# A small extra store of the first K block into the output, early in a linear attention kernel

## The chip, the cores and the metric

The kernel runs on one core of a Trainium2 chip. The metric is the device time of one execution in microseconds (us). A core has five engines with instruction queues of their own: TensorE (PE in the profile, with its weight loads as PEld), VectorE (DVE), ScalarE (ACT), GpSimd (POOL) and SyncE (SP). Data moves between the device memory (HBM) and the on-chip memory (SBUF) by 16 DMA engines. In this kernel SyncE and GpSimd issue the transfers; the profile lists those of SyncE under the queue q1 (hardware_dynamic) and those of GpSimd under q0 (software_dynamic).

## The reference

Linear attention without a mask, for 8 x 12 = 96 heads of 512 positions with 64 values each, all in float32:

```python
Q_feat = np.maximum(0, Q) + 1
K_feat = np.maximum(0, K) + 1
KV = np.einsum('bhkd,bhkv->bhdv', K_feat, V)
K_sum = np.sum(K_feat, axis=2)
numerator = np.einsum('bhqd,bhdv->bhqv', Q_feat, KV)
denominator = np.einsum('bhqd,bhd->bhq', Q_feat, K_sum)
return numerator / (denominator[:, :, :, None] + 1e-10)
```

Q, K, V and the output have 12.58 MB each, so 37.75 MB are read and 12.58 MB written.

## The kernel before

The 49,152 rows of 64 values are cut into blocks. A block of K or V has 128 partitions of 32 rows (8 heads). Two such blocks and the Q rows that belong to them make what the code calls a pair: 16 heads, and there are six of them, numbered s = 0 to 5. For each pair and each of its blocks n = 0, 1 the work is:

- `load` (line 135): GpSimd issues a DMA that reads K or V as float32 and writes bf16 tiles; `load_q` (line 131) does the same for Q. One exception is the first K block: `load_first_k` (line 125) lets SyncE load it in float32, as it is, into a buffer of the output pool `out_pool`, which nothing else uses yet.
- `k_features` (line 156): VectorE makes the K features, and `v_block` (line 169) on VectorE or ScalarE puts the V rows into a block layout with a column of ones, so that sums and products come out of one matmul.
- `keys_values` (line 181): 32 matmuls sum up KV and K_sum in PSUM; `weights` (line 194) brings them to SBUF as bf16.
- `q_features` (line 173), `transposes` (line 203) and `transposed` (line 210): Q features, transposed on TensorE and copied out.
- `out_matmuls` (line 215) and `norms` (line 229): the output matmuls, then a reciprocal (line 234) and a product (line 235) on VectorE into an output tile `o_sb`, in eight parts for each pair.
- `store` (line 148): the output tile goes to HBM. The stores of pairs 0 to 4 are issued by GpSimd, those of pair 5 by SyncE in three pieces.

The order on each engine is written out by hand in `ORDER` (line 23). A word there is a task: `lv2` is the load of V for pair 2, `s00` the first store of pair 0, `n31` part 1 of the norms of pair 3. GpSimd's list and SyncE's list are these:

```python
    POOL="""
        lv2 lk2 lq2 lv3 lq3 lk3 lq4 lv4 lk4 lv5 lq5 lk5 s00 s20 s10 s30 s40 s41
    """,
    SP="""
        s50 s51 s52
    """,
```

The loads of pairs 0 and 1 stand ahead of these lists, in the main part of the kernel (line 359 on). It begins with the first K block on SyncE, then V on GpSimd, then a few constants and the other loads. Semaphores are placed by the framework: an instruction waits for whatever last wrote what it reads, and for whoever last used the place that it writes. Output buffers rotate: `out_pool` has `OUT_BUFS` = 4, the first K block takes the first of them, pairs 0, 1 and 2 the next three, and pair 3 comes back to the first. `o_dram` (line 85) is the output seen as 128 partitions x 48 blocks x 8 rows x 64 values; eight of the 48 blocks belong to a pair.

Of the kernel before, what the change touches and what calls it, by code (L numbers as in the profile page):

```python
# [20 lines left out]
    k="kv", t="tr", m="om", f="kf", v="vb", q="qf", n="no", c="tc", e="ev", s="st"  # L21
# [32 lines left out]
def kernel(  # L54
# [12 lines left out]
    nc = tc.nc  # L67
# [11 lines left out]
    def view(t, c):  # L79
        return t.flatten_outer_dims().rearrange("(n p c) d -> p n c d", p=P, c=c)  # L80
# [4 lines left out]
    o_dram = view(out, C)  # L85
# [29 lines left out]
    raw = {}  # L115
# [9 lines left out]
    def load_first_k():  # L125
        t = out_pool.tile([P, 8, C, D], FP32, name="o_sb")
        t = t.rearrange("p a c d -> p (a c) d")[:, 0:ROWS]
        nc.sync.dma_start(out=t, in_=k_dram[:, 0])
        raw["k", 0, 0] = t

    def load_q(s):
        raw["q", s] = pools["q"].tile([P, QROWS, D], BF16, name="q_raw")
        nc.gpsimd.dma_start(out=raw["q", s], in_=q_dram[:, s])  # L133

    def load(x, s, ns=(0, 1)):
        if x == "q":
            load_q(s)
            return
        if (x, s) not in tiles:
            tiles[x, s] = pools[x].tile([P, 2, ROWS, D], BF16, name=f"{x}_raw")  # L140
        t = tiles[x, s]
        nc.gpsimd.dma_start(  # L142
            out=t[:, ns[0] : ns[-1] + 1], in_=drams[x][:, 2 * s + ns[0] : 2 * s + ns[-1] + 1]
        )
        for n in ns:
            raw[x, s, n] = t[:, n]
# [95 lines left out]
    def masks():  # L242
        nc.vector.tensor_scalar(out=odd, in0=lane, scalar1=16, scalar2=None, op0=ALU.bitwise_and)
        nc.vector.tensor_scalar(
            out=least[:, 0:1], in0=odd, scalar1=-1.0 / 16, scalar2=1.0, op0=ALU.mult, op1=ALU.add
        )
        nc.vector.tensor_scalar(
            out=least[:, 1:2], in0=odd, scalar1=1.0 / 16, scalar2=None, op0=ALU.mult
        )
        nc.vector.tensor_scalar(  # L250
            out=shift, in0=least, scalar1=-1.0, scalar2=-LOWEST, op0=ALU.add, op1=ALU.mult
        )
        nc.vector.tensor_tensor(out=shift, in0=shift, in1=least, op=ALU.add)

    def clear(i):
        t = v_alls[i].rearrange("p c x -> p (c x)").bitcast(FP32)
        w = t.shape[1] * 5 // 8
        nc.vector.memset(t[:, 0:w], 0.0)  # L258
        nc.scalar.copy(out=t[:, w:], in_=zero.to_broadcast([P, t.shape[1] - w]))  # L259
        nc.vector.tensor_copy(  # L260
            out=v_alls[i].rearrange("p c (b d) -> p c b d", b=4)[:, :, :, D],
            in_=ones[:, None, :].to_broadcast([P, ROWS, 4]),
        )
# [79 lines left out]
    def read(word):  # L343
        if word[0] == "l":
            return ("load", int(word[2]), word[1])
        return (TASKS[word[0]], *map(int, word[1:]))

    def trace_all(orders):

        left = {engine: list(tasks) for engine, tasks in orders.items()}  # L350
        while any(left.values()):
            before = len(done)
            for engine, tasks in left.items():
                while tasks and all(t in done or t[1] < 0 for t in needs(engine, tasks[0])):
                    trace(engine, tasks[0])
                    done.add(tasks.pop(0))
            assert len(done) > before, {e: t[:1] for e, t in left.items()}

    with tc.manual_schedule():
        nc.vector.memset(zero, 0.0)  # L360
        load_first_k()
        load("v", 0, (0,))
        nc.gpsimd.iota(lane, pattern=[[0, 1]], base=0, channel_multiplier=1)
        load("k", 0, (1,))
        load("v", 0, (1,))
        load("q", 0)
        nc.vector.memset(ones, 0.0)
        for b in range(4):
            nc.vector.memset(ones[32 * b : 32 * b + 32, b : b + 1], 1.0)
        clear(0)  # L370
        masks()
        make_identity(nc, identity)
        for t in kva_rows:
            nc.scalar.copy(out=t.bitcast(FP32), in_=zero.to_broadcast([P, 8 * W]))  # L374
        for x in "kvq":
            load(x, 1)
        clear(1)
        for s in range(2):
            done.update(("load", s, x) for x in "kvq")
        trace_all({engine: [read(x) for x in text.split()] for engine, text in ORDER.items()})  # L380
# [30 lines left out]
```

## Time and profile before

| what | value |
|---|---|
| time, median of 3 runs (lowest, highest) | 125.58 us (125.2, 126.08) |
| the profiled execution: time / span | 125.6 us / 123.8 us |
| mean granted TensorE clock | 0.901 |
| busy over the span | PE 83.0 us (67%), PEld 62.7 (51%), DVE 89.7 (72%), ACT 89.3 (72%), POOL 18.6 (15%) |
| HBM read and written | 37.75 MB and 12.58 MB |
| first load of K, issued by SyncE | at 0.74 us, lands after 4.8 us |
| loads issued by GpSimd | from 1.28 to 72.45 us |
| stores issued by GpSimd | from 73.47 to 108.73 us |
| stores issued by SyncE | from 112.10 to 115.46 us |

The profile shows one execution; its span runs from the first instruction to the last, and the rest of its time lies outside. A time in a slice row is given as a digit, the busy share in tenths, 40 slices over the span. The DMA row is the mean busy share of the 16 DMA engines, and the row GB/s what they moved, counted at the destination.

### The profile page before, as it was taken

The numbers are of one execution on the slowest core, as the hardware profiler recorded it, in microseconds if no ns is written. First come the engines' busy times: TensorE is split into PE (matmuls) and PEld (weight loads), VectorE is DVE, ScalarE is ACT, GpSimd is POOL, SyncE is SP. The second block draws the span as 40 slices with busy tenths as digits, with TensorE's granted clock in tenths as the row PEclk, the third lists the DMA queues.
The fourth block names the chain that finished last, engine by engine and source line by source line (L and its number), as shares of the span: only waits on it lengthen the run. The fifth ranks groups of instructions, "written<-read, shape, count | busy, mean of one in ns | idle before, by whom it ended". The sixth has DMA issues, their size and how long they took to land.

```text
span 123.8 us, 2306 instructions
## 1 busy us (share of the span) xinstructions
PE 83.0 (67%) x960; PEld 62.7 (51%) x960; DVE 89.7 (72%) x167; ACT 89.3 (72%) x99; POOL 18.6 (15%) x32
## 2 busy tenths in 40 slices
PE   0000396881998957999919998399984999976000
PEld 0000275851676835688716776277853677654000
DVE  4795429609699599969569992999959789789200
ACT  7959914939969999399999559999992996540000
POOL 6900000600003200140000090050000200220000
PEclk9999999999599997699995999999999599997555
DMA  3999999999999999999999999999999999999992
GB/s 85 339 212 212 217 214 217 213 232 220 192 212 217 229 209 209 214 220 210 220 226 198 213 217 216 213 226 202 214 327 417 419 413 418 417 413 417 409 407 100
DMA packets 7897, 32.11 MB, mean 259 GB/s; under 512 B 464, under 2 KB 464, under 8 KB 6992
## 3 DMA queue, kind: packets, MB, share of 16 engines
q0 software_dynamic: 6672, 28.84, 93.6%
q1 hardware_dynamic: 1216, 3.15, 6.8%
q8 instruction: 7, 0.11, 0.3%
q14 instruction: 2, 0.02, 0.0%
HBM read 37.75 MB, written 12.58 MB: 406 GB/s over the span
## 4 chain that ended last, share of the span: by engine, by line
DMA 44%; DVE 14%; PE 14%; ACT 13%; issue 4%; POOL 3%; POOLq 0%
DMA k_raw<-in_K_dram 32%; DMA q_raw<-in_Q_dram 12%; PE kva_ps L186 10%; DVE o_sb L235 7%; ACT v_all L171 6%; ACT qt L213 5%; DVE kf L159 4%; PE o_ps L221 3%; ACT kva L198 2%; POOL v_raw L142 2%; DVE v_all L171 2%; DVE recip L234 1%; PE qt_ps L206 1%; DVE qf L175 1%; POOL q_raw L133 0%
## 5 line engine op out<-in xcount | busy, mean ns | idle before, releaser
L186 PE MATMUL kva_ps<-v_all,kf 128*128 128x260 bf16 x384 | 55.2, 297 | 20.7 <-DVE v_all L171 17.7
L186 PEld LDWEIGHTS <-kf 128*128 128x128 bf16 x384 | 37.7, 105 | 31.1 <-DVE v_all L171 16.3
L171 ACT COPY v_all<-v_raw 32x2048 bf16<-32x2048 bf16 x22 | 42.3, 1929 | 6.9 <-DMA v_raw<-in_V_dram 5.1
L235 DVE TENSOR_TENSOR o_sb<-o_ps,recip 128x512 f32<-128x512 f32 x48 | 33.2, 692 | 1.7
L213 ACT COPY qt<-qt_ps 128x1024 bf16<-128x1024 bf16 x24 | 23.5, 1014 | 10.9 <-PE qt_ps L206 8.3
L221 PE MATMUL o_ps<-kva,qt 128*64 128x130 bf16 x384 | 20.6, 238 | 9.6 <-DVE o_sb L235 9.0
L159 DVE TENSOR_SCALAR kf<-k_raw,shift,least 128x2048 bf16<-128x2048 bf16 x22 | 16.9, 810 | 8.0 <-DMA k_raw<-in_K_dram 8.0
L221 PEld LDWEIGHTS <-qt 128*64 128x64 bf16 x384 | 13.3, 116 | 18.0 <-DVE o_sb L235 11.9
L171 DVE COPY v_all<-v_raw 32x2048 bf16<-32x2048 bf16 x26 | 18.0, 692 | 5.9 <-DMA v_raw<-in_V_dram 5.3
L198 ACT CAST kva<-kva_ps 64x260 bf16<-64x260 f32 x48 | 17.9, 374 | 3.7 <-PE kva_ps L186 2.9
L206 PE MATMUL qt_ps<-identity,qf 128*128 128x128 bf16 x192 | 14.0, 220 | 1.1 <-ACT qt L213 0.6
L206 PEld LDWEIGHTS <-qf 128*128 128x128 bf16 x192 | 12.0, 99 | 2.5 <-issue 0.8
L142 POOL DMA_DIRECT2D v_raw<-in_V_dram x7 | 4.9, 701 | 49.1 <-ACT qt L213 18.1
L234 DVE RECIPROCAL recip<-o_ps 128x8 f32<-128x8 f32 x48 | 9.6, 201 | 3.2 <-PE o_ps L221 3.0
L175 DVE TENSOR_SCALAR qf<-q_raw 128x4096 bf16<-128x4096 bf16 x6 | 7.3, 1223 | 4.7 <-DMA q_raw<-in_Q_dram 4.6
L150 POOL DMA_DIRECT2D out_dram<-o_sb x6 | 5.1, 853 | 30.9 <-DVE o_sb L235 23.6
L258 DVE MEMSET v_all<- 128x2600 f32 x2 | 4.5, 2225 | 1.1 <-issue 1.1
L133 POOL DMA_DIRECT2D q_raw<-in_Q_dram x6 | 3.5, 580 | 10.5 <-DVE recip L234 10.5
L142 POOL DMA_DIRECT2D k_raw<-in_K_dram x6 | 4.5, 746 | 0.0
L259 ACT COPY v_all<-zero 128x1560 f32<-128x1560 f32 x2 | 3.0, 1488 | 0.0
L159 DVE TENSOR_SCALAR kf<-o_sb,shift,least 128x2048 bf16<-128x2048 f32 x2 | 2.6, 1358 | 0.0
L374 ACT COPY kva<-zero 128x1040 f32<-128x1040 f32 x2 | 2.0, 1052 | 0.0
(17 smaller groups left out, 4.6 us busy)
## 6 DMA issues: line engine op xcount, KB each, us to landing
out_dram<-o_sb POOLq DMA_DIRECT2D x4, 2048.0 KB, 22.8
q_raw<-in_Q_dram POOLq DMA_DIRECT2D x6, 1024.0 KB, 17.4
k_raw<-in_K_dram POOLq DMA_DIRECT2D x5, 1024.0 KB, 19.9
v_raw<-in_V_dram POOLq DMA_DIRECT2D x5, 1024.0 KB, 15.7
out_dram<-o_sb POOLq DMA_DIRECT2D x2, 1024.0 KB, 10.0
o_sb<-in_K_dram SPq DMA_DIRECT2D x1, 1024.0 KB, 4.8
v_raw<-in_V_dram POOLq DMA_DIRECT2D x2, 512.0 KB, 8.5
out_dram<-o_sb SPq DMA_DIRECT2D x1, 1024.0 KB, 8.3
```

Of the source, the lines that this page charges most:

```text
L142: nc.gpsimd.dma_start(out=t[:, ns[0] : ns[-1] + 1], in_=drams[x][:, 2 * s + ns[0] : 2 * s + ns[-1] + 1])
L150: engine.dma_start(out=o_dram[:, 8 * s + lo : 8 * s + hi], in_=outs[s][:, lo:hi], single_packet=engine is nc.gpsimd,)
L159: nc.vector.tensor_scalar(out=kf[:, :, a], in0=raw["k", s, n], scalar1=shift[:, a : a + 1], scalar2=least[:, a : a + 1], op0=ALU.add, op1= ...
L171: copy(out=v_alls[n][ps, :, b * D1 : b * D1 + D], in_=raw["v", s, n][ps])
L175: nc.vector.tensor_scalar(out=qf.rearrange("p r c d -> p (r c) d"), in0=raw["q", s], scalar1=1.0, scalar2=1.0, op0=ALU.add, op1=ALU.max,)
L186: nc.tensor.matmul(kva_pss[s, n], lhsT=kfs[s, n][:, c].rearrange("p a d -> p (a d)"), rhs=v_alls[n][:, c], start=(c == 0), stop=(c == ROWS ...
L198: nc.scalar.copy(out=kvas[s % 2][64 * x : 64 * x + 64, 8 * n + a : 8 * n + 8 : 2, x], in_=kva_ps[64 * a : 64 * a + 64].rearrange("p (b d) ...
L206: nc.tensor.transpose(qt_ps[:, r], qfs[s][:, r, 2 * i : 2 * i + 2].rearrange("p x d -> p (x d)"), identity)
L213: copy(out=qts[s][:, i], in_=qt_pss.pop((s, i)).rearrange("p r q -> p q r"))
L221: nc.tensor.matmul(o_ps[64 * t : 64 * t + 64, c // 2, (c % 2) * W : (c % 2) * W + W], lhsT=qts[s][:, c, 8 * h : 8 * h + 8], rhs=kvas[s % 2 ...
L234: nc.vector.reciprocal(out=recip, in_=cells[:, :, :, D:D1])
L235: nc.vector.tensor_tensor(out=outs[s][:, part].rearrange("p (b r) d -> p b r d", b=2), in0=cells[:, :, :, 0:D], in1=recip.to_broadcast([P, ...
```

## The change

One line is added in the main part of the kernel, behind the first two loads. SyncE issues a DMA that copies from SBUF to the output: 16 partitions of the first K block, two rows of 64 float32 values from each, 512 B in one piece, 8 KB in all. The destination is partitions 0 to 15, block 0, rows 0 and 1 of the output, which belong to pair 0; what stands there is replaced when pair 0's own store writes the whole block.

```diff
         nc.vector.memset(zero, 0.0)
         load_first_k()
         load("v", 0, (0,))
+        nc.sync.dma_start(out=o_dram[0:16, 0, 0:2], in_=raw["k", 0, 0][0:16, 0:2])
         nc.gpsimd.iota(lane, pattern=[[0, 1]], base=0, channel_multiplier=1)
         load("k", 0, (1,))
         load("v", 0, (1,))
```

The instructions of the changed program differ from those before in these places alone: SyncE has the new DMA, which waits for the load of the first K block; GpSimd's store of pair 0 (line 150) waits for the new DMA; and one product on VectorE (line 235), the first into the output tile of pair 3, waits for it too. The order of all other instructions on each engine is as it was.

## The prediction

> **What bounds the kernel now.** I read first the 40 slices of the span, to see whether any engine or the transfers are full all the time; then the stretches, to see how full, and where that begins and ends; then the queues and the DMA issues, to price one packet and to find landing times. The slices:
>
> ```profile
> DVE  4795429609699599969569992999959789789200
> ACT  7959914939969999399999559999992996540000
> DMA  3999999999999999999999999999999999999992
> GB/s 85 339 212 212 217 214 217 213 232 220 192 212 217 229 209 209 214 220 210 220 226 198 213 217 216 213 226 202 214 327 417 419 413 418 417 413 417 409 407 100
> ```
>
> VectorE and ScalarE have holes in many slices; the DMA row is at 9 in all but the first and the last. The table by stage sharpens this (columns: the stretch in us, its length, busy us and instructions of PE, PE weight loads, DVE, ACT and POOL, the granted clock, the DMA share, GB/s):
>
> ```profile
> 0.00:3.00 3.00, 0.00 (x0) 0.00 (x0) 1.43 (x7) 2.25 (x2) 1.83 (x8) 1.00 0.35 74
> 3.00:20.00 17.00, 5.14 (x36) 3.79 (x37) 10.57 (x16) 11.76 (x9) 3.22 (x7) 1.00 1.05 238
> 60.00:80.00 20.00, 15.11 (x177) 11.30 (x175) 14.99 (x27) 16.78 (x19) 3.35 (x4) 0.91 1.05 214
> 95.00:115.00 20.00, 17.74 (x220) 12.53 (x216) 17.60 (x41) 12.13 (x18) 2.42 (x3) 0.87 1.02 415
> 115.00:121.00 6.00, 0.00 (x0) 0.00 (x0) 0.43 (x1) 0.00 (x0) 0.00 (x0) 0.50 1.03 406
> 121.00:122.00 1.00, 0.00 (x0) 0.00 (x0) 0.00 (x0) 0.00 (x0) 0.00 (x0) 0.50 0.52 201
> 122.00:123.80 1.80, 0.00 (x0) 0.00 (x0) 0.00 (x0) 0.00 (x0) 0.00 (x0) 0.50 0.02 9
> ```
>
> From 3 to 121 us the 16 DMA engines are full (a share of 1.02 to 1.05). The last compute instruction ends at 114.74 + 0.69 = 115.4 us, and 6 us of queued transfers still run behind it. The two rates are one limit seen twice: the loads are counted by the bf16 that they write, so 214 GB/s written is about 430 GB/s read, while a store counts the same on both sides and shows 415. A wait on a compute engine therefore costs nothing unless it leaves the DMA engines without work; what costs time is anything that occupies a DMA engine. The queue's own prices:
>
> ```profile
> DMA packets 7897, 32.11 MB, mean 259 GB/s; under 512 B 464, under 2 KB 464, under 8 KB 6992
> q0 software_dynamic: 6672, 28.84, 93.6%
> q1 hardware_dynamic: 1216, 3.15, 6.8%
> ```
>
> **The change, part by part.** Nothing is removed. One DMA is added on SyncE's queue, and two waits come with it: the real store of the first pair must follow the early one (same place in the output), and the tile that held the first K block must not be written again before the early store has read it.
>
> *SyncE.* The early store needs the first K block, so SyncE waits for that load: issued at 0.74 us, landing 4.8 us later, at 5.54 us. One issue takes 0.37 to 0.39 us by SyncE's four rows. SyncE has nothing else until its first output store at 112.10 us, so the wait and the issue cost nothing; the cover is over 100 us. No load is issued by SyncE behind it: all others go through GpSimd, which does not wait for SyncE here.
>
> *The transfer.* 16 rows of 512 B, 8 KB, in q1. The count of small packets tells how a DMA ends: 464 packets under 512 B for 29 DMAs (25 issued by GpSimd, 4 by SyncE) are 16 for each, one for each DMA engine. So I expect 16 data packets and 16 small ones more in q1 (1248), one pair to each engine. Their price is not in the trace alone, so I bound it. Below: the bytes only, 512 B at one engine's share of the store rate, 415/16 = 26 GB/s, 0.02 us. Above: two mean packets of q1, each 6.8% of 16 x 123.8 us over 1216 packets = 0.11 us for 2.6 KB, so 0.22 us. I take 0.1 us, nearer to the bytes of a 512 B row plus one small packet than to two packets five times its size. It arrives when the engines are full, and since they stay full to the end, it lies wholly on the path: +0.1 us, between 0.02 and 0.22.
>
> *GpSimd.* The wait is put before the first pair's real store, issued at 73.47 us. Behind it on GpSimd stand the other five stores (the next at 81.74 us); all loads have been issued by then. The early store is issued at about 5.9 us. Even if it took the longest landing of any store in this trace, 25.3 us, it would be done at 31.2 us, 42 us ahead. The wait is a passed one: at most one more semaphore instruction, 17 ns by the rows of such instructions on GpSimd's queue: nothing.
>
> *VectorE.* The load's tile is one of four output buffers, so the fourth pair's first product into it now waits for the early store too. That product is the 25th of its kind and starts at 81.59 us; again satisfied tens of microseconds before. Whoever waits for it (the TensorE result buffers) sees 21 ns at most, which the 6 us of queued transfers at the end hide.
>
> *The end.* SyncE waits at the end for its DMAs one by one; one more that is long done is one more short semaphore instruction (17 to 28 ns by that group's minimum and median), before the last landing and so hidden.
>
> *Sum.* 125.6 us for the profiled execution (span 123.8, 1.8 outside it), plus 0.1, is 125.7 us. That execution stands at the median of the runs shown, 125.58, so the forecast carries over as it is: 125.7, no change that could be told. About 1%, 1.26 us, is what a measurement of this kernel separates from no change; the three runs alone span 0.9 us.
>
> **The rivals.**
>
> *The engines stand still for the confirmation of the write (slower).* If an engine moved nothing between writing its row to the output and having that write confirmed, all 16 would pause once, at about 7 us, with full queues behind them. The price by rows: at the end the traffic falls by half in the stretch from 121 to 122, and the last store, issued at 115.46 with the shortest landing of 7.5 us, is complete at 123.0; so some 1.5 us pass between the middle of the last bytes and the confirmation. The time would be 125.6 + 1.5 = 127.1 us; it decides for slower from a pause of 1.26 us. Against it: four stores land between 95 and 115 us (the first three pairs' and the fourth's, from their issue at 73.47 to 97.44 us and landings of 15.5 to 25.3 us). Four such pauses would take 6 of these 20 us, but the rate there is 415 GB/s. Against the loads' best 437 GB/s read, at most 5% is missing, 1 us, or 0.25 us for a store. So this rival lives only if a lone small store behaves otherwise: 0.06. The Trainium skill, page "DMA: Bandwidth & Descriptors", section "Anatomy of one DMA", fits a DMA's time as about 2.0 us fixed plus its bytes at 436 GB/s, with most of the 2.0 us the wait for the write's receipt; taken as occupied time that would be an estimate of 2.02 us and a sum of 127.6 us. By that rule read as latency only, nothing is added, and the stretch at 415 GB/s agrees with the reading as latency.
>
> *The rows don't spread (slower).* If all 16 rows went to one DMA engine, it would carry up to 16 x 0.11 = 1.8 us more than the others, everything that needs that engine's share of a load or store would come later, and the full engine would end last: 127.4 us. It decides from 12 rows on one engine (1.26/0.11), and only at the upper price of a packet; at 0.02 us it would be 0.3 us. For it: no DMA of 16 rows is in the trace, all have 128. Against it: each of the 29 ended with 16 small packets. 0.06. The Trainium skill, page "DMA: Bandwidth & Descriptors", section "Why a DMA increments its semaphore by 16 and not by 1", says that the number of engines is the largest one up to 16 that divides the outermost sizes of both sides; 16 and 16 give 16 engines here and the sum without this rival. No run here shows a transfer of that shape yet.
>
> *The early write helps later stores (faster).* The output's first write would then come when nothing waits for it, and the later stores would run at the loads' rate: 12.58 MB at 415 GB/s take 30.3 us, at 437 GB/s 28.8, so 1.5 us less, 124.1 us. Against it: there is no sign of a first-use price. SyncE's three stores were issued in 372 to 387 ns, like its load in 377; the stores run at 413 to 419 GB/s from the first full slice to the last but two, without a slow start. Apart from this only about 3 us before the engines are full and 2 us after the last bytes are free, and the change touches neither. 0.05.
>
> **How the numbers follow.** No change to tell: 0.83, at 125.7 us. Slower by over 1%: 0.06 + 0.06 = 0.12. Faster: 0.05. The range takes the spread of the runs shown, 125.2 to 126.08, moves it by the bounds of the added transfer, 0.02 to 0.25 us (the upper one from the missing 5%), and adds 0.2 us at each end, since three runs do not show the ends of a spread: 124.9 to 126.5. The 0.17 of the other cases lies mostly outside it, and that is within what may be left out.
>
> **What would show each step.** q1 with 1248 packets and 8 KB more, and 480 small packets in all; SyncE with one more issue of about 0.38 us near 5.6 us, and its landing a few microseconds on; GpSimd's first store at about 73 us with no wait for SyncE's transfer ahead of it; the DMA share still at 1.0 or above in every stretch from 3 to 121 us, the stretch from 5 to 9 us too; the last bytes at about 122 us. A share or a rate that dips between 6 and 9 us by over 1 us of traffic would show the first rival; a tail of a few per cent at the end, longer than the 0.02 after 122 us, the second; store slices above 420 GB/s the third. The prediction is wrong if any of these moves the end by more than 1.26 us, or if loads begin to be issued later than before and leave the DMA engines empty in between.

## The result and the profile after

| | before | after |
|---|---|---|
| time, median of 22 runs each (lowest to highest) | 125.51 us (125.11 to 126.08) | 125.75 us (125.54 to 126.12) |
| ratio after to before, 95% interval | | 1.0024 (1.0013 to 1.0034) |
| span, mean of the runs | 123.71 us (85 runs) | 123.78 us (22 runs) |
| time less span, mean of the runs | 1.78 us (85 runs) | 1.99 us (22 runs) |

The change costs 0.24%, about 0.30 us (0.16 to 0.43); that is the difference of the means, the medians differ by 0.24 us. The last two rows split it: the span of each run is known to 0.1 us, so single differences mean little, but the mean of time less span is steady (the runs scatter by 0.03 us). The 85 runs of the kernel before are those beside the experiments below; they come in four groups, whose mean spans lay between 123.66 and 123.75 us. So the span grew by about 0.07 us, no more than the groups differ among themselves, and what lies outside it by 0.20 us.

The page of the kernel after, where the prediction named what to look for:

```profile
span 123.5 us, 2308 instructions
...
DMA packets 7929, 32.12 MB, mean 260 GB/s; under 512 B 480, under 2 KB 496, under 8 KB 7024
...
q0 software_dynamic: 6672, 28.84, 93.9%
q1 hardware_dynamic: 1248, 3.15, 6.9%
```

q1 has 32 packets more: 16 small ones (464 to 480 under 512 B) and 16 of 512 B, which now stand alone between the limits of 512 B and 2 KB (480 to 496). The queue q0 is unchanged. This execution's span is even shorter than that of the one shown before, although the kernel is slower: one execution can't show a difference of 0.3 us here.

The stages after (columns as before: stretch, length, busy us and instructions of PE, PE weight loads, DVE, ACT, POOL, granted clock, DMA share, GB/s):

```profile
6.00:9.00 3.00, 0.00 (x0) 0.00 (x0) 2.90 (x3) 1.47 (x2) 0.29 (x1) 1.00 1.08 214
95.00:115.00 20.00, 17.69 (x222) 12.42 (x216) 17.59 (x41) 12.14 (x18) 2.42 (x3) 0.87 1.02 415
115.00:121.00 6.00, 0.00 (x0) 0.00 (x0) 0.48 (x1) 0.00 (x0) 0.00 (x0) 0.50 1.03 405
121.00:122.00 1.00, 0.00 (x0) 0.00 (x0) 0.00 (x0) 0.00 (x0) 0.00 (x0) 0.50 0.59 229
122.00:123.80 1.80, 0.00 (x0) 0.00 (x0) 0.00 (x0) 0.00 (x0) 0.00 (x0) 0.50 0.03 10
```

The stretch from 6 to 9 us, where the early store runs, was this before:

```profile
6.00:9.00 3.00, 0.00 (x0) 0.00 (x0) 2.90 (x3) 1.66 (x2) 0.29 (x1) 1.00 1.06 212
```

So there is no dip there (1.08 and 214 GB/s against 1.06 and 212), the rate in the store phase is the same, and there is no long tail. On SyncE the store is issued where it was expected (start, us, line; the last row, of the three output stores, adds up their time), and the list of issues has its landing (KB each, median us from issue to landing):

```profile
0.75 0.39 SPq L128 DMA_DIRECT2D o_sb<-in_K_dram  x1
5.82 0.35 SPq L363 DMA_DIRECT2D out_dram<-o_sb  x1
112.15 3.73 SPq L150 DMA_DIRECT2D out_dram<-o_sb  x3
```

```profile
out_dram<-o_sb SPq DMA_DIRECT2D x1, 8.0 KB, 4.6
```

It lands after 4.6 us, at 10.4 us; GpSimd's first store is issued at 73.59 us. What is left is a small thing on VectorE. The rows of line 235, the products that write the output tiles, before and then after (columns: what it is, how often, shortest, median and longest duration in ns, first and last start):

```profile
L235 DVE TENSOR_TENSOR o_sb<-o_ps,recip x48: 691/691/693, 29.3 to 114.7; 128x512 f32<-128x512 f32 x48
L235 DVEq EVENT_SEMAPHORE  x2: 21/21/21, 98.4 to 108.6; - x2
```

```profile
L235 DVE TENSOR_TENSOR o_sb<-o_ps,recip x48: 690/691/693, 29.6 to 114.8; 128x512 f32<-128x512 f32 x48
L235 DVEq EVENT_SEMAPHORE  x3: 21/21/21, 80.9 to 108.7; - x3
```

The added wait of the 25th product, which starts at 81.70 us, stands ahead of it as an instruction of its own, 21 ns long, at 80.9 us. So the trace has two instructions more (2306 to 2308): SyncE's DMA, and one on VectorE, 182 in place of 181.

### The profile page after: what moved, and what is told of

It reads as the page before. It is cut to its first block, busy times and chain, and to the rows that moved or that the text cites. A ratio compares the mean times of both kernels' runs of the same rounds, so it can differ in the third digit from the quotient of the medians.

```text
span 123.5 us, 2308 instructions
## 1 busy us (share of the span) xinstructions
PE 83.0 (67%) x960; PEld 62.7 (51%) x960; DVE 89.5 (72%) x167; ACT 89.4 (72%) x99; POOL 18.6 (15%) x32
## 4 chain that ended last, share of the span: by engine, by line
DMA 44%; DVE 14%; PE 14%; ACT 13%; issue 4%; POOL 3%; POOLq 0%
DMA k_raw<-in_K_dram 32%; DMA q_raw<-in_Q_dram 12%; PE kva_ps L186 10%; DVE o_sb L235 7%; ACT v_all L171 6%; ACT qt L213 5%; DVE kf L159 4%; PE o_ps L221 3%; ACT kva L198 2%; POOL v_raw L142 2%; DVE v_all L171 2%; DVE recip L234 1%; PE qt_ps L206 1%; DVE qf L175 1%; POOL q_raw L133 0%
```

## The experiments

Each kernel has runs of the kernel before beside it, on the same chip. "Outside" is the mean of time less span over the runs; beside the experiments it was 1.78 to 1.80 us in the kernel before. "VectorE instructions" are those of the trace, waits of their own included.

| run | ratio (95% interval) | span, mean (before beside it) | VectorE instructions | outside, us |
|---|---|---|---|---|
| the change | 1.0024 (1.0013 to 1.0034) | 123.78 | 182 | 1.99 |
| e1: eight early stores | 1.0049 (1.0038 to 1.0061) | 124.23 (123.71) | 185 | 1.80 |
| e2: 128 rows in one store | 1.0043 (1.0030 to 1.0056) | 123.94 (123.71) | 182 | 1.99 |
| e3: into SBUF | 1.0022 (1.0011 to 1.0034) | 123.75 (123.71) | 182 | 1.99 |
| e4: pair 5's place | 1.0019 (1.0007 to 1.0032) | 123.73 (123.71) | 182 | 1.98 |
| f1: a load, no wait | 1.0003 (0.9986 to 1.0020) | 123.78 (123.75) | 181 | 1.78 |
| f2: one VectorE memset more, no store | 1.0024 (1.0008 to 1.0039) | 123.84 (123.75) | 182 | 2.00 |
| f3: the change and that memset | 1.0032 (1.0019 to 1.0045) | 123.82 (123.75) | 183 | 2.14 |
| f4: the change, last stores merged | 1.0026 (1.0014 to 1.0038) | 123.83 (123.75) | 182 | 1.99 |
| g1: three memsets more, no store | 1.0030 (1.0017 to 1.0042) | 123.65 (123.68) | 184 | 2.16 |
| g2: the change and three memsets | 1.0001 (0.9990 to 1.0012) | 123.76 (123.68) | 185 | 1.78 |
| g3: two copies more on ScalarE | 0.9999 (0.9986 to 1.0012) | 123.70 (123.68) | 181 | 1.78 |
| h1: one memset moved off VectorE | 1.0019 (1.0006 to 1.0033) | 123.70 (123.66) | 180 | 1.99 |

### Does the cost grow with the transfer?

```diff
-        nc.sync.dma_start(out=o_dram[0:16, 0, 0:2], in_=raw["k", 0, 0][0:16, 0:2])
+        for j in range(8):
+            nc.sync.dma_start(out=o_dram[0:16, j, 0:2], in_=raw["k", 0, 0][0:16, 0:2])
```

> Eight early stores of 16 rows x 512 B to eight blocks of pair 0, in place of one. The one store cost 0.24% (0.13 to 0.34), about 0.30 us. Theory P (each data packet and each small packet occupies a full DMA engine): eight times the cost, 8 x 0.30 = +2.4 us (1.3 to 3.4) over the kernel before. Theory F (a fixed price for each DMA, whatever its size): also +2.4 us. Theory B (bytes alone, as the low end of the prediction's bounds): 8 x 0.02 = +0.16 us. Theory O (a single disturbance of the first loads, not a price of the transfer): about +0.3 us as with one store.

```diff
-        nc.sync.dma_start(out=o_dram[0:16, 0, 0:2], in_=raw["k", 0, 0][0:16, 0:2])
+        nc.sync.dma_start(out=o_dram[:, 0, 0:2], in_=raw["k", 0, 0][:, 0:2])
```

> One early store of 128 rows x 512 B: the same bytes and data packets as the eight stores, but one DMA. Theory P: eight data packets and one small one for each engine; if both kinds cost the same 0.15 us, 9 x 0.15 = +1.35 us (0.7 to 1.9). Theory F: as one store, +0.3 us, plus bytes (64 KB at 415 GB/s, 0.16 us), +0.3 to 0.45 us. Theory B: +0.16 us. Theory O: about +0.3 us.

The packets came as meant. The page of the kernel with eight stores, then that of the kernel with 128 rows:

```profile
DMA packets 8153, 32.18 MB, mean 259 GB/s; under 512 B 592, under 2 KB 720, under 8 KB 7248
```

```profile
DMA packets 8041, 32.18 MB, mean 260 GB/s; under 512 B 480, under 2 KB 608, under 8 KB 7136
```

Both have 128 packets of 512 B (720 less 592, 608 less 480); the eight DMAs have 128 small packets more than the kernel before, the one DMA 16. Measured were 0.49% and 0.43%, about 0.6 and 0.5 us. With eight stores that is neither the 2.4 us of P and F nor the bytes alone, and not the 0.3 us of O; with 128 rows it is below the range of P, and only F comes near (0.3 to 0.45 us). No theory fitted both, since eight times the transfer cost only about twice as much. The spans tell why it could look so: they grew by 0.53 and 0.23 us, while outside the span e2 has the change's 1.99 us and e1 the old 1.80. The 0.30 us from which P, F and O were reckoned mixed two costs.

Of the spans alone one price follows: 0.53/8 = 0.07 us for each small store. With d for a data packet and s for a small one on each engine, 8d + 8s = 0.53 and 8d + s = 0.23 give s = 0.04 and d = 0.02 us; with mean spans that are uncertain by some 0.05 us, these are rough. The eight stores also have eight times as many DMAs as the one, so s may as well be a price for each DMA; these two runs can't tell one from the other. In the profiled execution with eight stores the last bytes come later, as a price on full engines should show:

```profile
6.00:9.00 3.00, 0.00 (x0) 0.00 (x0) 2.90 (x3) 1.55 (x2) 0.29 (x1) 1.00 1.08 216
...
121.00:122.00 1.00, 0.00 (x0) 0.00 (x0) 0.00 (x0) 0.00 (x0) 0.00 (x0) 0.50 0.71 274
122.00:123.80 1.80, 0.00 (x0) 0.00 (x0) 0.00 (x0) 0.00 (x0) 0.00 (x0) 0.50 0.09 34
```

From 121 us on the DMA share is 0.71 and 0.09 (and 0.66 and 0.07 with 128 rows), against 0.59 and 0.03 with the change and 0.52 and 0.02 before. The five kernels without an added transfer have 0.47 to 0.52 and 0.00 to 0.03 there, the seven with a single transfer of 8 KB 0.50 to 0.61 and 0.02 to 0.05: the eight stores stand out, one store hardly does.

### The write, and the waits that came with it

The first run writes into a tile of the kernel that nothing uses, the second to a place of the output that belongs to pair 5.

```diff
-    head.tile([P, HEAD], FP32, name="spacer")
+    spare = head.tile([P, HEAD], FP32, name="spacer")
...
-        nc.sync.dma_start(out=o_dram[0:16, 0, 0:2], in_=raw["k", 0, 0][0:16, 0:2])
+        nc.sync.dma_start(
+            out=spare[0:16, 0:128].rearrange("p (c d) -> p c d", d=D), in_=raw["k", 0, 0][0:16, 0:2]
+        )
```

> The same 16 rows at the same time on the same queue, written into an unused SBUF tile instead of the output: no HBM write, no wait for GpSimd's store; the wait on VectorE stays. If the cost is the write into HBM or GpSimd's wait: 0.0 us, ratio 1.000. If it is packets on full engines, whatever their target (P, F), or a disturbance by any transfer (O): +0.3 us, ratio 1.0024 (1.0013 to 1.0034).

```diff
-        nc.sync.dma_start(out=o_dram[0:16, 0, 0:2], in_=raw["k", 0, 0][0:16, 0:2])
+        nc.sync.dma_start(out=o_dram[0:16, 40, 0:2], in_=raw["k", 0, 0][0:16, 0:2])
```

> The same store to the place of pair 5, which SyncE itself stores at the end: GpSimd's first store no longer waits. If GpSimd's wait is the cost: ratio 1.000. If it is the transfer (P, F, O): 1.0024 (1.0013 to 1.0034), as with the change.

Both cost what the change costs, 1.0022 and 1.0019. So neither the write into HBM nor the wait of GpSimd's first store is the cause. Both runs kept VectorE's wait, and both have 1.98 to 1.99 us outside the span.

### VectorE's program or SyncE's DMAs?

Here the theories are V (the share outside hangs on VectorE's program) and S (it hangs on SyncE's DMAs or the semaphores in use). The first run has no early store, but a load of the same size into the tile `spare` of above; SyncE issues it at 1.20 us and nobody waits for it:

```diff
         load("v", 0, (0,))
+        nc.sync.dma_start(
+            out=spare[0:16, 0:128].rearrange("p (c d) -> p c d", d=D), in_=k_dram[0:16, 0, 0:2]
+        )
```

> The share outside the span (time less span) is 1.78 us in the kernel before, 1.98 us with the one early store, 1.98, 1.98 and 1.97 us with 128 rows, the SBUF target and pair 5's place, but 1.80 us with eight stores. Here SyncE gets a fifth DMA (16 rows x 512 B of K from HBM into the unused tile) that nobody waits for, right behind its first load: VectorE has no added instruction (181 in the trace), SyncE one DMA and one end semaphore more. Theory V (the share outside hangs on VectorE's program, 182 instructions against 181 or 185): 1.78 us outside, and +0.02 to 0.1 us in the span. Theory S (it hangs on SyncE's number of DMAs or on the semaphores in use, 17 against 16): 1.98 us outside.

```diff
         nc.vector.memset(zero, 0.0)
+        nc.vector.memset(zero, 0.0)
         load_first_k()
```

> The kernel before, with one VectorE instruction of 0.06 us more (a second memset of the zero tile, 182 VectorE instructions) and no DMA more. Theory V: 1.98 us outside the span, ratio 1.0016, the span as before. Theory S: 1.78 us outside, ratio 1.000.

The third run has the early store and this memset:

> The changed kernel, with the same VectorE instruction more (183). Theory V with a parity or a block that is full again: 1.78 us outside and a ratio of about 1.0008, the early store's own 0.1 us alone; if V counts from a limit, 1.98 us outside. Theory S: 1.98 us outside, ratio 1.0024.

The fourth has the early store, and SyncE's last two stores as one:

```diff
-        s50 s51 s52
+        s50 s51
...
-        return (range(4), range(4, 8)) if s < last else (range(4), range(4, 6), range(6, 8))
+        return (range(4), range(4, 8)) if s < last else (range(4), range(4, 8))
```

> The changed kernel, with the last two stores of SyncE made one (parts 4 to 7 in one store of 1 MB): SyncE has four DMAs and 16 semaphores are in use, as before the change, and VectorE keeps 182 instructions. Theory V: 1.98 us outside the span. Theory S: 1.78 us outside. The span may change at its end by the later start of the merged store; six us of queued stores should hide it, so 0 to +0.3 us.

Theory S misses in all four runs, theory V in one. A fifth DMA of SyncE without an instruction on VectorE leaves 1.78 us (f1), one short memset on VectorE without any DMA gives 2.00 us and the whole ratio of the change (f2), and four DMAs of SyncE with 182 instructions on VectorE give 1.99 us (f4). The added memset is 59 ns long and starts at 0.9 us, where VectorE has time to spare:

```profile
L361 DVE MEMSET zero<- x1: 59/59/59, 0.9 to 0.9; 128x1 f32 x1
```

f3 went on to 2.14 us: neither the 1.98 us of S nor the 1.78 or 1.98 us that V had for it, but another step.

### Does it go round?

e1 had 185 instructions on VectorE, since four of the added waits stand there as instructions of their own, and 1.80 us. So the steps had to come back somewhere.

```diff
-        nc.vector.memset(zero, 0.0)
+        for _ in range(4):
+            nc.vector.memset(zero, 0.0)
         load_first_k()
```

> The share outside the span was 1.78 us at 181 VectorE instructions in the trace, 1.99 at 182, 2.14 at 183 and 1.80 at 185 (there with eight stores besides). Here the kernel before gets three more memsets of the zero tile on VectorE (184) and nothing else. Theory V4 (the share goes round with four instructions): 184 is the one step not seen; if it keeps climbing, 2.2 to 2.35 us; if it falls back before 185, near 1.6 to 1.8. Theory L (it grows with the number, and the eight stores hid it): 2.3 us. The span as before, 123.7 to 123.9.

The same three memsets, with the early store kept:

> The changed kernel with three more memsets of the zero tile on VectorE (185). Theory V4: 1.78 us outside the span as in the kernel before, so that only the early store's own cost in the span is left: ratio 1.000 to 1.0008, although three instructions were added to the changed kernel. Theory L: 2.4 us outside, ratio 1.005.

And on ScalarE:

```diff
             nc.scalar.copy(out=t.bitcast(FP32), in_=zero.to_broadcast([P, 8 * W]))
+        for _ in range(2):
+            nc.scalar.copy(out=kva_rows[0].bitcast(FP32)[:, 0:1], in_=zero)
```

> The kernel before with two more copies of one column on ScalarE (one or two instructions more in its program, as one wait becomes needless), VectorE at 181. If the share outside hangs on VectorE's program alone: 1.78 us. If any engine's program that grows by one or two instructions does it: 1.98 us or another step away from 1.78.

The changed kernel with three useless instructions more is back at the time before, 1.0001 (0.9990 to 1.0012). At 184 the share is 2.16 us, at 185 1.78. Two instructions more on ScalarE change nothing. From 181 to 185 the steps are 1.78, 1.99, 2.14, 2.16, 1.78. They come back at 185 as V4 has it, and against L, which had 2.3 us at 184 and 2.4 at 185; 2.16 us at 184 is a little under the 2.2 to 2.35 that V4 gave for a climb. Its test below that range:

```diff
-        nc.vector.memset(zero, 0.0)
+        nc.gpsimd.memset(zero, 0.0)
         load_first_k()
```

> The kernel before with the memset of the zero tile moved from VectorE to GpSimd: VectorE has 180 instructions in the trace, one less. The share outside the span was 1.78 us at 181, 1.99 at 182, 2.14 at 183, 2.16 at 184 and 1.78 at 185. Theory V4 (it goes round with four instructions): 180 stands where 184 stands, 2.16 us, so that taking an instruction away makes the kernel slower by 0.38 us, ratio 1.003; the span as before or 0.1 us more, as GpSimd issues its first load 0.1 us later. Rival (only added instructions cost): 1.78 us or less, ratio 1.000 to 1.001.

1.99 us, not the 2.16 of V4, and not the 1.78 of its rival. An instruction less on VectorE does cost time, but by another step than a round of four gives. GpSimd has one instruction more in this run (59 for 58), which was not tried by itself. In e1 GpSimd has 62 in the trace, and the share is the same there as in g2 with 58 (1.80 and 1.78 us, VectorE at 185 in both), which speaks against GpSimd's number. The rule of the steps stays open.

## Why the prediction was right, and what it missed

The forecast was 125.7 us, no change that could be told, in a range of 124.9 to 126.5; measured were 125.75 us. The main reading holds: the DMA engines bound the kernel, and of the two rivals on the slower side nothing is seen. That the two numbers agree to 0.05 us is luck. The one execution from which the sum started, 125.6 us, stood 0.09 us above the median of the 22 runs before, and the change cost 0.24 to 0.30 us in place of 0.1. The limit of 1.26 us for what can be told was too wide as well: over 22 runs each, the interval of the ratio leaves 1.000 out. The range by its own terms begins at 125.0 us, not at 124.9 (125.2 + 0.02 - 0.2).

**The transfer.** Sixteen data packets and sixteen small ones, as expected. The price of 0.1 us, between 0.02 and 0.22, stands against 0.07 us by the eight stores. The spans with a single small transfer can't confirm it: they grew by 0.02 to 0.08 us, and f2, which has no DMA more, by 0.09. The data packet comes out near the lower bound of the prediction, its bytes at the store rate (0.02 us); the rest, 0.04 us, goes with the small packet or with the DMA as a whole.

**The pause for the write's confirmation.** Eight stores cost 0.53 us in the span, so no store lets the engines stand for 1.5 us, and writing into SBUF in place of HBM saves nothing (e3). The Trainium skill, page "DMA: Bandwidth & Descriptors", section "Anatomy of one DMA", has about 2.0 us fixed for each DMA, by a fit of transfers that GpSimd issues; the early store is issued by SyncE. As latency this is not refuted here, since the early store landed 4.6 us after its issue, but as occupied time even one store would have cost 2.0 us, and the eight cost 0.53 us together.

**The rows on one engine.** There are 16 more small packets, as many as there are engines, and the tail after 122 us has a share of 0.03, within the 0.00 to 0.03 of the kernels without an added transfer. The trace does not name the engine of a packet, so that the rows spread is inferred from these. The rule of the Trainium skill, page "DMA: Bandwidth & Descriptors", section "Why a DMA increments its semaphore by 16 and not by 1", by which 16 and 16 rows give 16 engines, agrees with both numbers.

**Later stores helped.** From 95 to 115 us the rate is 415 GB/s in both. One slice of the page after reads 424 GB/s, beside 309 in the slice ahead of it (327 before): a shift of bytes by one slice, not a gain. (Of the slices before, those of the stores read 413 to 419 only up to the last but three; the prediction had it up to the last but two, which is 409.) g2, which has the early store and a share outside of 1.78 us, stands at 1.0001 (0.9990 to 1.0012): no gain of 1.5 us either.

**The step that failed** is the sum, together with VectorE's part: "span 123.8, 1.8 outside it", taken as fixed, and "21 ns at most". The added wait became an instruction of its own, as long as foreseen and hidden in the span as foreseen. But the share outside the span went from 1.78 to 1.99 us with it, and this 0.20 us is most of the measured 0.30 us. That the number of instructions on VectorE and not the store is the cause is shown from both sides: one instruction more without the store (f2), a transfer of the same size without the instruction (f1, a load), the store with three instructions more (g2). The further semaphore instruction that the prediction had at SyncE's end did not come; there are ten in both traces.

Why the share steps so is not shown. The views of the profile cover the span alone. The kept traces also hold updates of semaphores outside it, and in the two executions shown those of the semaphore that is updated on both sides lie alike to 2 ns from 0.37 us ahead of the span to the last one, 1.90 us behind it, although time less span is 1.77 us in the one and 1.99 in the other. So no delay of 0.20 us is seen close to either end of the span. Other runs give no pattern: in g1 the last four updates come 0.38 us later, in f3, with nearly the same share, 0.03 us. Whether the share grows ahead of the first instruction or behind the last one stays open.

## What to carry to other kernels

Where the DMA engines are full from end to end, price an added transfer by its packets on each engine, here roughly 0.02 us for 512 B and 0.04 us for the end of each DMA, and leave its latency out unless somebody waits for it. Compare time less span as well as the span: a difference of some tenths of a microsecond may lie wholly outside what the profile shows. And before a part of a change is blamed for such a difference, undo its effect on the length of an engine's program: here three idle instructions took away 0.2 us that looked like the price of a store. That other kernels have such steps is not shown.

## What was not expected of the hardware

In this kernel the time outside the span went with the number of VectorE's instructions in the trace, in steps of one instruction: 1.78 us at 181, 1.99 at 182, 2.14 at 183, 2.16 at 184 and 1.78 at 185, each steady to 0.02 to 0.04 us from run to run, whatever the instruction was (a semaphore wait in the middle, a memset at the start). Two instructions more on ScalarE did nothing. With 180 on VectorE and one more on GpSimd it was 1.99 us. The same number gave the same share in different programs: six at 182 lay between 1.98 and 2.00 us, two at 185 at 1.78 and 1.80.
